# Loading the last 128 positions as tiles of 64 positions of two batches, masked by batch, with the second 64 positions scanned last

## The chip, the cores and the metric

The kernel runs on one core of one Trainium2 chip. The metric is the device time of an execution in microseconds, as the median of several; the executions of one kernel in one set agree within 0.15%. A profile's span, from the first to the last instruction, is 1.8 us shorter than the time in the kernel before. Ratios are the mean time of one kernel's fast runs over that of the other's fast runs in the same rounds, so they are not quite the ratio of the medians quoted.

## The reference

```python
B, S, D = 8, 2048, 4096              # x: [B, S, D] fp32, w: [D, 1] fp32
proj = (x @ w).squeeze(-1)           # [8, 2048]
cm = np.maximum.accumulate(proj, axis=1)
is_record = (proj >= cm).astype(np.float32)
return np.cumsum(is_record, axis=1)
```

x has 268 MB and each element is used once: a stream. Maximum and count run along the positions, so the last positions can only be finished once everything before them is.

## The kernel before

Positions 0 to 1919 come in four groups of 4, 4, 4 and 3 times 128 positions, the first three in a loop. In a group, each of the eight batches has a tile of 128 partitions with 4 (or 3) rows of 16 KB each. DVE takes the dot product of the first 2816 columns of a row, POOL multiplies the other 1280 by w and ACT sums them. Matmuls against the identity turn the sums into rows of positions, and DVE scans them. The last 128 positions follow as one tile per batch, the last two batches cut in pieces so that little work is left when the last bytes land.

```python
identity = sb([P, P], "identity")                 # 512 bytes per partition
small = sb([P, 352], "small")                     # 1408
w2 = sb([P, WC], "w2")                            # 2048
xall = sb([P, NS * R * D], "xall")                # 196608: three slots of 4 rows of 16 KB
xbuf = [xall[:, i * R * D : (i + 1) * R * D] for i in range(NS)]
w_sb = sb([P, PC], "w_sb")
# ... cm, cnt, cm_l, cnt_l (the last two 512 bytes each)

# the last two batches: batch, columns loaded, DVE's columns, POOL's columns
PIECES = [
    (1, 1408, D, (1408, VC), (VC, D)),
    # ... six pieces cut ...
    (0, 160, 448, (160, 448), None),
    (0, 0, 160, (0, 160), None),
]

def row_load(m, c0, c1, b, done):                 # one batch, 128 positions
    u, xb = slot(m)
    i = SY.dma_start(out=xb[:, c0:c1], in_=x[b, S0:, c0:c1]).then_inc(done, 16)
    # ... waits until the slot is free ...

with V.Fori(0, NL):                               # NL = 3
    next_group()
    group_dots(R)
next_group()
group_dots(RS[-1], NL)

# the end
        if i == len(PIECES) - 1:
            V.wait_ge(pa, na)                     # all of ACT's sums are there
# ...
V.tensor_reduce(out=fin, in_=accs, op=ALU.add, axis=mybir.AxisListType.X)
# ... matmuls of 128 columns into ps ...
scans(cm_l, cnt_l, P, cm[:, n - 1 : n], cnt[:, n - 1 : n], 4)
SY.dma_start(out=out[:, S0:], in_=cnt_l)
```

Of the kernel before, what the change touches and what calls it, by code (L numbers as in the profile page):

```python
# [13 lines left out]
ALU = mybir.AluOpType  # L14
ACTF = mybir.ActivationFunctionType
# [5 lines left out]
def kernel(  # L21
# [16 lines left out]
    P = 128  # L38
    B, S, D = x.shape
    WC = 512  # L40
    NW = D // WC
    RS = (4, 4, 4, 3)
    R = RS[0]
    NS = 3
    NG = len(RS)
    NL = NG - 1
    N = R * P
    STARTS = [sum(RS[:g]) * P for g in range(NG)]
    S0 = sum(RS) * P
    assert S0 + P == S  # L50
    VC = 2816
# [1 line left out]
    CV = 3584  # L53


    PIECES = [
        (1, 1408, D, (1408, VC), (VC, D)),
        (1, 0, 1408, (0, 1408), None),
        (0, 2816, D, (2816, 3328), (3328, D)),
        (0, 2048, 2816, (2048, 2816), None),  # L60
        (0, 1280, 2048, (1600, 2048), (1280, 1600)),
        (0, 832, 1280, (832, 1280), None),
        (0, 448, 832, (448, 832), None),
        (0, 160, 448, (160, 448), None),
        (0, 0, 160, (0, 160), None),
    ]
    W2 = 1280

    pool = ctx.enter_context(tc.tile_pool(name="sb", bufs=1))
    wpool = ctx.enter_context(  # L70
# [3 lines left out]
    def sb(shape, name, **kw):  # L74
        return pool.tile(shape, FP32, name=name, **kw)

    identity = sb([P, P], "identity")
    small = sb([P, 352], "small")
    w2 = sb([P, WC], "w2")
    xall = sb([P, NS * R * D], "xall")  # L80
    xbuf = [xall[:, i * R * D : (i + 1) * R * D] for i in range(NS)]
    w_sb = sb([P, PC], "w_sb")
    cm = sb([B, N], "cm")
    cnt = sb([B, N], "cnt")
    cm_l, cnt_l = (sb([B, P], n) for n in ("cm_l", "cnt_l"))
    w_v = wpool.tile([P, CV], FP32, name="w_v")
    ps = wpool.tile([P, WC], FP32, name="ps")
    w_row = w2[:NW, :]

    off = [0]  # L90

    def cut(n):
        off[0] += n
        assert off[0] <= 352
        return small[:, off[0] - n : off[0]]

    sum_v, sum_p = cut(R * B), cut(R * B)
    st_v, st_p = cut(B), cut(B)
    b1x = cut(B)
    accs = cut(2 * len(PIECES))  # L100
    acc_v, acc_p = accs[:, : len(PIECES)], accs[:, len(PIECES) :]
    fin = cut(1)
    neg = cut(1)[:B]

# [2 lines left out]
    def sem(name):  # L107
        return tc.alloc_semaphore(f"{name}_{next(ns)}")

    rows = [b for b in reversed(range(B)) if b > 1]  # L110
    xs = [sem("xs") for _ in range(B)]
    fr = [sem("fr") for _ in range(B)]
    xt = [sem("xt") for _ in rows]
    xq = [sem("xq") for _ in PIECES]
    ws, idn, bw, wc, cs, od, oe, psr, pd, pl, go, sd, pa, con = (
        sem(n) for n in "ws idn bw wc cs od oe psr pd pl go sd pa con".split()
    )

    V, A, G, T, SY = nc.vector, nc.scalar, nc.gpsimd, nc.tensor, nc.sync

    def dot(xsl, wsl, dst):
        return V.tensor_tensor_reduce(  # L122
            out=xsl, in0=xsl, in1=wsl, scale=1.0, scalar=0.0,
            op0=ALU.mult, op1=ALU.add, accum_out=dst,
        )
# [4 lines left out]
    def w_pool(c0, c1):  # L130
        if c0 >= VC:
            return w_sb[:, c0 - VC : c1 - VC]
        assert W2 <= c0 and c1 <= W2 + WC
        return w2[:, c0 - W2 : c1 - W2]

    def scans(cm_, cnt_, n, cm0, cnt0, base=1):
        low = neg.to_broadcast([B, n])
        V.tensor_tensor_scan(  # L138
            out=cm_, data0=ps[:B, :n], data1=low, initial=cm0, op0=ALU.max, op1=ALU.max,
        )._wait_ge(psr, base).then_inc(psr, 1)  # L140
        V.tensor_tensor(  # L141
            out=ps[:B, :n], in0=ps[:B, :n], in1=cm_, op=ALU.is_ge
        )._wait_ge(psr, base + 1).then_inc(psr, 1)
        V.tensor_tensor_scan(  # L144
            out=cnt_, data0=ps[:B, :n], data1=low, initial=cnt0, op0=ALU.add, op1=ALU.max,
        )._wait_ge(psr, base + 2).then_inc(cs, 1)

    def at(g, t):
# [9 lines left out]
    with tc.tile_critical(no_gpsimd_drain=True):  # L158

        for g in range(NG):  # L160
            r = RS[g]
            for t in range(B):
                i = SY.dma_start(
                    out=at(g, t)[:, : r * D],
                    in_=x[B - 1 - t, STARTS[g] : STARTS[g] + r * P, :].rearrange(
                        "(p r) d -> p (r d)", r=r
                    ),
                ).then_inc(xs[t], 16)
# [12 lines left out]
        def slot(m):  # L181
            if m < NS:
                return None, xbuf[m][:, RS[-1] * D :]
            u = B - NS if m < 2 * NS else B - NS + 1
            return u, at(NL, u)[:, (m % NS) * D : (m % NS + 1) * D]

        freed = {None}

        def row_load(m, c0, c1, b, done):
            u, xb = slot(m)  # L190
            i = SY.dma_start(  # L191
                out=xb[:, c0:c1], in_=x[b, S0:, c0:c1]
            ).then_inc(done, 16)
            if u not in freed:
                freed.add(u)
                i._wait_ge(fr[u], 2 * NG)

        for m, b in enumerate(rows):
            row_load(m, 0, D, b, xt[m])
        for i, (b, c0, c1, _, _) in enumerate(PIECES):  # L200
            row_load(B - 1 - b, c0, c1, b, xq[i])
            if i == 3:
                SY.dma_start(
                    out=out[:, STARTS[-1] : S0], in_=cnt[:, : S0 - STARTS[-1]]
                )._wait_ge(cs, NG + 1).then_inc(oe, 16)
# [22 lines left out]
        A.copy(out=w_sb[:, : CV - VC], in_=w_v[:, VC:CV])._wait_ge(bw, NW).then_inc(  # L228
            wc, 1
        )  # L230
        A.copy(out=w2, in_=w_v[:, W2 : W2 + WC]).then_inc(wc, 1)  # L231
        A.sem_inc(od, 32)


        V.memset(cm[:, N - 1 :], NEG)
        V.memset(cnt[:, N - 1 :], 0.0)
        V.wait_ge(con, 3)
# [3 lines left out]
        def group_scans(r=R):  # L241
            V.wait_ge(od, 16)
            n = r * P
            scans(cm[:, :n], cnt[:, :n], n, cm[:, N - 1 :], cnt[:, N - 1 :])

        def group_dots(r, g=0):
            for t in range(B):
                b, xb = B - 1 - t, at(g, t)
                V.wait_ge(xs[t], 16).then_inc(go, 1)
                V.sem_inc(xs[t], -16)  # L250
                for j in range(r):
                    i = dot(
                        xb[:, j * D : j * D + VC], w_v[:, :VC],
                        sum_v[:, j * B + b : j * B + b + 1],
                    )
                i.then_inc(fr[t], 1)

        def next_group():
            group_scans()
            V.sem_inc(psr, -3)  # L260
            V.sem_inc(od, -16)

        with V.Fori(0, NL):
            next_group()
            group_dots(R)
        next_group()
        group_dots(RS[-1], NL)

# [41 lines left out]
                        i.then_inc((pd, psr)[k], 1)  # L310


        nv = npool = na = 0
        parts = []

        def piece(xb, v, p, dst_v, dst_p, landed):
            nonlocal nv, npool, na
            dot(xb[:, v[0] : v[1]], w_v[:, v[0] : v[1]], dst_v)._wait_ge(
                landed, 16
            ).then_inc(sd, 1)  # L320
            nv += 1
            if p:
                xl = xb[:, p[0] : p[1]]
                G.tensor_mul(out=xl, in0=xl, in1=w_pool(*p))._wait_ge(  # L324
                    landed, 16
                ).then_inc(pl, 1)
                npool += 1
                add_up(xl, dst_p)._wait_ge(pl, npool).then_inc(pa, 1)
                na += 1

        for m, b in enumerate(rows):
            piece(
                slot(m)[1], (0, VC), (VC, D), st_v[:, b : b + 1], st_p[:, b : b + 1],
                xt[m],
            )
            if m == 0:
                group_scans(RS[-1])
        for i, (b, c0, c1, v, p) in enumerate(PIECES):
            if b == 1:
                dst_v, dst_p = (b1x if p is None else st_v)[:, 1:2], st_p[:, 1:2]  # L340
            else:
                dst_v, dst_p = acc_v[:, i : i + 1], acc_p[:, i : i + 1]
            piece(slot(B - 1 - b)[1], v, p, dst_v, dst_p, xq[i])
            if i == len(PIECES) - 1:
                V.wait_ge(pa, na)
            if i == 1:
                parts += [(B, st_v, (sd, nv)), (B, b1x, None), (B, st_p, (pa, na))]
        V.tensor_reduce(  # L348
            out=fin, in_=accs, op=ALU.add, axis=mybir.AxisListType.X
        )._wait_ge(sd, nv).then_inc(sd, 1)  # L350
        nv += 1
        parts.append((1, fin, (sd, nv)))
        for k, (m, l, wait) in enumerate(parts):
            i = T.matmul(  # L354
                out=ps[:m, :P], lhsT=l[:, :m], rhs=identity,
                start=k == 0, stop=k == len(parts) - 1,
            )
            if wait:
                i._wait_ge(*wait)
        i.then_inc(psr, 1)  # L360
        n = RS[-1] * P
        scans(cm_l, cnt_l, P, cm[:, n - 1 : n], cnt[:, n - 1 : n], 4)
        SY.dma_start(out=out[:, S0:], in_=cnt_l)._wait_ge(cs, NG + 2).then_inc(oe, 16)
        G.wait_ge(oe, 16 * 2)


# [28 lines left out]
```

## Time and profile before

| what | value |
|---|---|
| time | 631.46 us, median of 3 runs (631.19 to 631.63) |
| span of the profile | 629.5 us |
| DMA | 268.55 MB, 427 GB/s over the span |
| busy: DVE, POOL, ACT | 65%, 59%, 28% |
| last piece of x complete | 624.14 us |
| output issued | 626.98 us |

These lines are of the page of the kernel before: its span; the mean busy share of the 16 DMA engines in 40 slices, in tenths; packets and bytes; and one group of instructions (line, engine, operation, operands, count, then busy us and the mean ns of one, then the idle time before it).

```profile
span 629.5 us, 1144 instructions
...
DMA  9999999999999999999999999999999999999995
...
DMA packets 6868, 268.55 MB, mean 427 GB/s; under 512 B 800, under 2 KB 1328, under 8 KB 1872
...
L138 DVE TENSOR_TENSOR_SCAN cm_l<-ps,cm,small 8x128 f32<-8x128 f32 x1 | 0.5, 470 | 0.7 <-PE ps L354 0.7
```

The DMA row says what bounds the kernel: in every slice but the last the DMA engines are busy for 90% or more, while the busiest compute engine has a third of the span to spare. The last line is one of the scans that the change halves: 470 ns for 128 columns.

The next lines are the timeline of the kernel before: start us, duration us, engine, line, operation, operands, and in brackets the idle time before it with what ended it. First one of POOL's products, that of the sixth of the last tiles, then the end.

```profile
614.22 2.90 POOL L324 TENSOR_TENSOR xall<-xall,w_sb 128x1280 f32<-128x1280 f32 x1 [1.94 <-DMA xall<-in_x_dram]
...
624.45 0.32 DVE L122 CUSTOM_DVE_ANT_0 xall<-xall,w_v 128x160 f32<-128x160 f32 x1
624.69 0.08 DVE L122 DVE_READ_ACCUMULATOR2_ANT small<- 128x1 f32 x1
624.80 0.17 DVE L348 TENSOR_REDUCE small<-small 128x1 f32<-128x18 f32 x1
625.03 0.09 PEld L354 LDWEIGHTS ps<-identity,small 128*1 128x1 f32 x2 [3.14 <-DVE small L348]
625.03 0.58 PE L354 MATMUL ps<-identity,small 128*1 128x128 f32 x2 [2.65 <-DVE small L348]
625.65 0.47 DVE L138 TENSOR_TENSOR_SCAN cm_l<-ps,cm,small 8x128 f32<-8x128 f32 x1 [0.68 <-PE ps L354]
626.15 0.29 DVE L141 TENSOR_TENSOR ps<-ps,cm_l 8x128 f32<-8x128 f32 x1
626.48 0.47 DVE L144 TENSOR_TENSOR_SCAN cnt_l<-ps,cnt,small 8x128 f32<-8x128 f32 x1
626.98 0.31 SPq L363 DMA_DIRECT2D out_dram<-cnt_l  x1
```

POOL waits for the load and starts as it lands (here 1.94 us of waiting, the last share at 614.15 us and the start at 614.22). The end is a chain of small steps.

The trace also records each DMA packet and each of the 16 shares in which a load lands (the last piece has 128 packets and 16 landings, so a share is taken to be what one DMA queue brings, eight partitions). A load is complete with its last share. For the last piece of x, the ninth of the 16 shares landed at 622.57 us and the last at 624.14: one queue ended 1.58 us behind the middle of the others. (In this text a "queue" is one of these 16.)

### The profile page before, as it was taken

To read this page: it belongs to the slowest core of one execution; us is meant where nothing else is said; L and a number is where in the kernel's file an instruction comes from. 1 tells how busy PE (TensorE), PEld (TensorE's weight loads), DVE (VectorE), ACT (ScalarE), POOL (GpSimd) and SP (SyncE) were. 2 spreads that over 40 slices of the span, in tenths; PEclk is the share of its full clock that TensorE was granted. 3 is DMA by queue.
4 is the path that set the end of the run, shared out by engine and by line. 5 is a ranking of instruction groups with operands and counts; after the bars stand their busy time and mean duration, and the time that the engine had idled before them with its cause. 6 is when DMAs were issued, how large, how long until landed. Compare 5 with 4: busy or idle time off the path is not lost.

```text
span 629.5 us, 1144 instructions
## 1 busy us (share of the span) xinstructions
PE 29.7 (5%) x84; PEld 13.2 (2%) x84; DVE 406.2 (65%) x292; ACT 177.8 (28%) x262; POOL 368.8 (59%) x137
## 2 busy tenths in 40 slices
PE   8000000000010000000020000000002000000101
PEld 3000000000000000000010000000001000000000
DVE  0755676456785557755579655677557966555887
ACT  1222332123322233222233222332222322322332
POOL 0555676456765557755567655577555966555855
PEclk9999999999975555555555555555555555555555
DMA  9999999999999999999999999999999999999995
GB/s 401 400 466 404 462 400 467 400 466 400 466 400 466 400 466 421 447 416 450 433 433 446 421 458 408 459 408 458 408 416 450 441 412 447 441 415 443 415 432 220
DMA packets 6868, 268.55 MB, mean 427 GB/s; under 512 B 800, under 2 KB 1328, under 8 KB 1872
## 3 DMA queue, kind: packets, MB, share of 16 engines
q1 hardware_dynamic: 6848, 268.50, 98.8%
q14 instruction: 4, 0.03, 0.0%
q10 hardware_dynamic: 16, 0.02, 0.0%
HBM read 268.45 MB, written 0.07 MB: 427 GB/s over the span
## 4 chain that ended last, share of the span: by engine, by line
POOL 52%; issue 37%; DMA 7%; PE 2%; DVE 1%; SPq 0%; POOLq 0%; ACT 0%; ACTq 0%
POOL xall L273 52%; DMA xall<-in_x_dram 6%; PE w_v L221 2%; DVE xall L122 0%; PE ps L221 0%; SPq L191 0%; DMA w<-in_w_dram 0%; POOLq L276 0%; ACT w L231 0%; PE ps L354 0%; DVE cm_l L138 0%; DVE cnt_l L144 0%; DVE ps L141 0%; ACT xall L128 0%; DVE small L348 0%
## 5 line engine op out<-in xcount | busy, mean ns | idle before, releaser
L122 DVE CUSTOM_DVE_ANT_0 xall<-xall,w_v 128x2816 f32<-128x2816 f32 (+3 forms) x135 | 388.7, 2931 | 187.8 <-DVEq L250 184.9
L273 POOL TENSOR_TENSOR xall<-xall,w_sb 128x1280 f32<-128x1280 f32 x120 | 344.8, 2905 | 246.0 <-POOLq L276 246.0
L128 ACT ACTIVATE xall<-xall 128x1280 f32<-128x1280 f32 x129 | 162.6, 1261 | 431.2 <-POOL xall L273 412.4
L303 PE MATMUL ps<-identity,small 128*8 128x128 f32 x60 | 13.4, 418 | 566.6 <-ACT xall L128 566.6
L324 POOL TENSOR_TENSOR xall<-xall,w_sb 128x1280 f32<-128x1280 f32 (+1 forms) x8 | 22.1, 2769 | 7.6 <-DMA xall<-in_x_dram 7.6
L128 ACT ACTIVATION_READ_ACCUMULATOR xall<-xall 128x1 f32 x129 | 24.1, 186 | 0.0
L303 PEld LDWEIGHTS ps<-identity,small 128*8 128x8 f32 x60 | 7.5, 131 | 573.6 <-ACT xall L128 569.7
L138 DVE TENSOR_TENSOR_SCAN cm<-ps,cm,small 8x512 f32<-8x512 f32 (+1 forms) x5 | 6.1, 1217 | 13.5 <-PE ps L303 13.4
L221 PE MATMUL w_v<-w,identity 8*128 8x512 f32 x14 | 12.2, 1056 | 0.0
L239 DVE MEMSET ps<- 8x512 f32 x1 | 0.5, 485 | 17.4 <-ACT w L231 17.4
L122 DVE DVE_READ_ACCUMULATOR2_ANT small<- 128x1 f32 x135 | 11.0, 81 | 0.0
L144 DVE TENSOR_TENSOR_SCAN cnt<-ps,cnt,small 8x512 f32<-8x512 f32 (+1 forms) x5 | 6.1, 1217 | 0.2
L221 PEld LDWEIGHTS w_v<-w,identity 8*128 8x128 f32 x14 | 4.6, 332 | 7.3 <-issue 7.3
L228 ACT COPY w_sb<-w_v 128x768 f32<-128x768 f32 x1 | 0.8, 798 | 11.4 <-PE w_v L221 11.4
L354 PE MATMUL ps<-identity,small 128*8 128x128 f32 (+1 forms) x8 | 2.2, 405 | 26.4 <-DVE small L122 23.8
L141 DVE TENSOR_TENSOR ps<-ps,cm 8x512 f32<-8x512 f32 (+1 forms) x5 | 3.3, 660 | 0.2
L221 PE MATMUL ps<-w,identity 8*128 8x512 f32 x2 | 2.1, 1137 | 2.9 <-DMA w<-in_w_dram 2.9
L227 ACT ACT_TABLE_LOAD x1 | 1.3, 1283 | 1.5 <-SPq L158 1.5
L227 ACT COPY w_sb<-ps 128x512 f32<-128x512 f32 x1 | 0.6, 585 | 2.2 <-PE ps L221 2.2
L354 PEld LDWEIGHTS ps<-identity,small 128*8 128x8 f32 (+1 forms) x8 | 0.6, 100 | 28.1 <-DVE small L122 24.3
L324 POOL TENSOR_TENSOR xall<-xall,w 128x320 f32<-128x320 f32 x1 | 0.9, 867 | 0.1
L138 DVE TENSOR_TENSOR_SCAN cm_l<-ps,cm,small 8x128 f32<-8x128 f32 x1 | 0.5, 470 | 0.7 <-PE ps L354 0.7
(15 smaller groups left out, 3.5 us busy)
## 6 DMA issues: line engine op xcount, KB each, us to landing
xall<-in_x_dram SPq DMA_DIRECT2D x8, 6144.0 KB, 33.4
xall<-in_x_dram SPq DMA_DIRECT2D x6, 2048.0 KB, 43.0
xall<-in_x_dram SPq DMA_DIRECT2D x1, 1344.0 KB, 37.7
xall<-in_x_dram SPq DMA_DIRECT2D x2, 384.0 KB, 31.1
xall<-in_x_dram SPq DMA_DIRECT2D x1, 704.0 KB, 39.0
xall<-in_x_dram SPq DMA_DIRECT2D x1, 640.0 KB, 40.0
xall<-in_x_dram SPq DMA_DIRECT2D x24, 44.9
xall<-in_x_dram SPq DMA_DIRECT2D x1, 224.0 KB, 22.6
```

The lines of the kernel that those rows point to most:

```text
L122: return V.tensor_tensor_reduce(out=xsl, in0=xsl, in1=wsl, scale=1.0, scalar=0.0, op0=ALU.mult, op1=ALU.add, accum_out=dst,)
L128: return A.activation(out=xsl, in_=xsl, func=ACTF.Copy, accum_out=dst)
L138: V.tensor_tensor_scan(out=cm_, data0=ps[:B, :n], data1=low, initial=cm0, op0=ALU.max, op1=ALU.max,)._wait_ge(psr, base).then_inc(psr, 1)
L141: V.tensor_tensor(out=ps[:B, :n], in0=ps[:B, :n], in1=cm_, op=ALU.is_ge)._wait_ge(psr, base + 1).then_inc(psr, 1)
L144: V.tensor_tensor_scan(out=cnt_, data0=ps[:B, :n], data1=low, initial=cnt0, op0=ALU.add, op1=ALU.max,)._wait_ge(psr, base + 2).then_inc(cs, 1)
L221: i = T.matmul(out=dst, lhsT=identity[:NW, k : k + 1].to_broadcast([NW, P]), rhs=w_row, start=True, stop=True,).then_inc(bw, 1)
L227: A.copy(out=w_sb[:, CV - VC :], in_=ps)._wait_ge(bw, 1).then_inc(wc, 1)
L228: A.copy(out=w_sb[:, : CV - VC], in_=w_v[:, VC:CV])._wait_ge(bw, NW).then_inc(wc, 1)
L273: i = G.tensor_mul(out=xl, in0=xl, in1=w_sb).then_inc(pl, 1)
L303: i = T.matmul(out=ps[:B, j : r * P : r], lhsT=l[:, j * B : (j + 1) * B], rhs=identity, start=k == 0, stop=k == 1,)
L324: G.tensor_mul(out=xl, in0=xl, in1=w_pool(*p))._wait_ge(landed, 16).then_inc(pl, 1)
L354: i = T.matmul(out=ps[:m, :P], lhsT=l[:, :m], rhs=identity, start=k == 0, stop=k == len(parts) - 1,)
```

## The change

Each of the last tiles now holds 64 positions of two batches in place of 128 positions of one. Tiles 0 to 3 bring the first 64 positions of all eight batches, so these can be scanned while the rest loads, and only 64 columns are left to scan at the end. A partition's sum has to go to the row of its own batch: it is multiplied by a mask of zeros and ones over the batches (by ACT, and for the last tile by DVE), and a matmul with a folded identity turns the two batches into rows of 64 columns. The pieces were cut anew (the last is 352 columns, not 160), and the third DVE group was taken out of the loop.

```diff
-    PIECES = [ ... nine pieces of batches 1 and 0 ... ]
-    W2 = 1280
+    H = 2
+    Q = P // H
+    LAST = [
+        (B - 2, 1696, D, (1696, VC), (VC, D)),
+        (B - 2, 0, 1696, (0, 1696), None),
+        (B - 1, 2592, D, (2592, 3552), (3552, D)),
+        (B - 1, 1440, 2592, (1792, 2592), (1440, 1792)),
+        (B - 1, 736, 1440, (736, 1184), (1184, 1440)),
+        (B - 1, 352, 736, (352, 736), None),
+        (B - 1, 0, 352, (0, 352), None),
+    ]
+    EARLY = 4
+    W2, W2C = 1184, 608
@@ the tiles in SBUF
     identity = sb([P, P], "identity")
     small = sb([P, 352], "small")
-    w2 = sb([P, WC], "w2")
+    masked = sb([P, 2 * P], "masked")
+    fold = sb([P, 2 * B - H + Q], "fold")
+    w2 = sb([P, W2C], "w2")
     xall = sb([P, NS * R * D], "xall")
@@ the loads
-                out=xb[:, c0:c1], in_=x[b, S0:, c0:c1]
+                out=xb[:, c0:c1],
+                in_=x[
+                    rows_of(m)[0] : rows_of(m)[0] + H,
+                    S0 + rows_of(m)[1] : S0 + rows_of(m)[1] + Q, c0:c1,
+                ].rearrange("b i d -> i b d"),
@@ DVE's groups
-        with V.Fori(0, NL):
+        with V.Fori(0, NL - 1):
             next_group()
             group_dots(R)
+        next_group()
+        group_dots(R)
         next_group()
         group_dots(RS[-1], NL)
@@ the masks
+        def by_batch(m, acc, start, stop, *wait):
+            ...
+            if m < B - 1:
+                A.activation(out=e, in_=on, func=ACTF.Copy, scale=acc)...
+            else:
+                V.tensor_tensor(out=e, in0=on, in1=acc.to_broadcast([P, B]), op=ALU.mult)...
+            return T.matmul(out=ps[:B, q : q + Q], lhsT=e, rhs=by_i, start=start, stop=bool(stop))...
@@ the end (cut)
-        scans(cm_l, cnt_l, P, cm[:, n - 1 : n], cnt[:, n - 1 : n], 4)
+        by_batch(B - 1, fin, False, True, sd, nv).then_inc(psr, 1)
+        ne = EARLY * H * Q // B
+        tail_scans(EARLY, B, cm_l[:, ne - 1 : ne], cnt_l[:, ne - 1 : ne], 7)
```

More of the change, by code (lines that the diff above doesn't have):

```diff
@@ L53, with rows_of @@
     CV = 3584
-    PIECES = [
-        (1, 1408, D, (1408, VC), (VC, D)),
-        (1, 0, 1408, (0, 1408), None),
-        (0, 2816, D, (2816, 3328), (3328, D)),
-        (0, 2048, 2816, (2048, 2816), None),
-        (0, 1280, 2048, (1600, 2048), (1280, 1600)),
-        (0, 832, 1280, (832, 1280), None),
-        (0, 448, 832, (448, 832), None),
-        (0, 160, 448, (160, 448), None),
-        (0, 0, 160, (0, 160), None),
-    ]
-    W2 = 1280
+    H = 2
[8 more added lines that the diff above has]
+        (B - 1, 0, 352, (0, 352), None),
+    ]
+    def rows_of(m):
+        return m * H % B, m * H // B * Q
+    TILES = [(m, 0, D, (0, VC), (VC, D)) for m in range(B - 2)] + LAST
+    NP = sum(q[0] == B - 1 for q in LAST)
+    EARLY = 4
+    W2, W2C = 1184, 608
     pool = ctx.enter_context(tc.tile_pool(name="sb", bufs=1))
@@ L87 @@
     ps = wpool.tile([P, WC], FP32, name="ps")
-    w_row = w2[:NW, :]
+    w_row = w2[:NW, :WC]
+    by_b, by_i = fold[:, : 2 * B - H], fold[:, 2 * B - H :]
     off = [0]
@@ L97 @@
     sum_v, sum_p = cut(R * B), cut(R * B)
-    st_v, st_p = cut(B), cut(B)
-    b1x = cut(B)
-    accs = cut(2 * len(PIECES))
-    acc_v, acc_p = accs[:, : len(PIECES)], accs[:, len(PIECES) :]
+    acc_v, acc_p = cut(B + 1), cut(B)
+    accs = cut(2 * NP)
     fin = cut(1)
@@ L108, in sem @@
         return tc.alloc_semaphore(f"{name}_{next(ns)}")
-    rows = [b for b in reversed(range(B)) if b > 1]
     xs = [sem("xs") for _ in range(B)]
     fr = [sem("fr") for _ in range(B)]
-    xt = [sem("xt") for _ in rows]
-    xq = [sem("xq") for _ in PIECES]
-    ws, idn, bw, wc, cs, od, oe, psr, pd, pl, go, sd, pa, con = (
-        sem(n) for n in "ws idn bw wc cs od oe psr pd pl go sd pa con".split()
+    xq = [sem("xq") for _ in TILES]
+    ws, idn, bw, wc, cs, od, oe, psr, pd, pl, go, sd, pa, con, fo, ms = (
+        sem(n) for n in "ws idn bw wc cs od oe psr pd pl go sd pa con fo ms".split()
     )
@@ L132, in w_pool, with scans @@
             return w_sb[:, c0 - VC : c1 - VC]
-        assert W2 <= c0 and c1 <= W2 + WC
+        assert W2 <= c0 and c1 <= W2 + W2C
         return w2[:, c0 - W2 : c1 - W2]
-    def scans(cm_, cnt_, n, cm0, cnt0, base=1):
-        low = neg.to_broadcast([B, n])
+    def scans(cm_, cnt_, src, cm0, cnt0, base=1):
+        low = neg.to_broadcast(list(src.shape))
         V.tensor_tensor_scan(
-            out=cm_, data0=ps[:B, :n], data1=low, initial=cm0, op0=ALU.max, op1=ALU.max,
+            out=cm_, data0=src, data1=low, initial=cm0, op0=ALU.max, op1=ALU.max,
         )._wait_ge(psr, base).then_inc(psr, 1)
         V.tensor_tensor(
-            out=ps[:B, :n], in0=ps[:B, :n], in1=cm_, op=ALU.is_ge
+            out=src, in0=src, in1=cm_, op=ALU.is_ge
         )._wait_ge(psr, base + 1).then_inc(psr, 1)
         V.tensor_tensor_scan(
-            out=cnt_, data0=ps[:B, :n], data1=low, initial=cnt0, op0=ALU.add, op1=ALU.max,
+            out=cnt_, data0=src, data1=low, initial=cnt0, op0=ALU.add, op1=ALU.max,
         )._wait_ge(psr, base + 2).then_inc(cs, 1)
@@ L187 @@
         freed = {None}
-        def row_load(m, c0, c1, b, done):
+        for i, (m, c0, c1, _, _) in enumerate(TILES):
             u, xb = slot(m)
-            i = SY.dma_start(
-                out=xb[:, c0:c1], in_=x[b, S0:, c0:c1]
-            ).then_inc(done, 16)
+            d = SY.dma_start(
+                out=xb[:, c0:c1],
[3 more added lines that the diff above has]
+                ].rearrange("b i d -> i b d"),
+            ).then_inc(xq[i], 16)
             if u not in freed:
                 freed.add(u)
-                i._wait_ge(fr[u], 2 * NG)
-        for m, b in enumerate(rows):
-            row_load(m, 0, D, b, xt[m])
-        for i, (b, c0, c1, _, _) in enumerate(PIECES):
-            row_load(B - 1 - b, c0, c1, b, xq[i])
-            if i == 3:
+                d._wait_ge(fr[u], 2 * NG)
+            if i == len(TILES) - 4:
                 SY.dma_start(
@@ L230 @@
         )
-        A.copy(out=w2, in_=w_v[:, W2 : W2 + WC]).then_inc(wc, 1)
+        A.copy(out=w2, in_=w_v[:, W2 : W2 + W2C]).then_inc(wc, 1)
         A.sem_inc(od, 32)
+        V.wait_ge(idn, 1)
+        V.memset(by_b, 0.0).then_inc(fo, 1)
+        V.wait_ge(fo, 1)
+        V.tensor_reduce(
+            out=by_b[:, B - H : B], in_=identity.rearrange("p (i b) -> p b i", b=H),
+            op=ALU.add,
+            axis=mybir.AxisListType.X,
+        )
+        V.tensor_reduce(
+            out=by_i, in_=identity.rearrange("p (i b) -> p i b", b=H), op=ALU.add,
+            axis=mybir.AxisListType.X,
+        ).then_inc(fo, 1)
+        V.wait_ge(fo, 2)
         V.memset(cm[:, N - 1 :], NEG)
@@ L243, in group_scans @@
             n = r * P
-            scans(cm[:, :n], cnt[:, :n], n, cm[:, N - 1 :], cnt[:, N - 1 :])
+            scans(cm[:, :n], cnt[:, :n], ps[:B, :n], cm[:, N - 1 :], cnt[:, N - 1 :])
         def group_dots(r, g=0):
@@ L310, with sums @@
                         i.then_inc((pd, psr)[k], 1)
-        nv = npool = na = 0
-        parts = []
-        def piece(xb, v, p, dst_v, dst_p, landed):
+        nv = npool = na = nm = 0
+        def sums(i, dst_v, dst_p):
             nonlocal nv, npool, na
+            m, _, _, v, p = TILES[i]
+            xb = slot(m)[1]
             dot(xb[:, v[0] : v[1]], w_v[:, v[0] : v[1]], dst_v)._wait_ge(
-                landed, 16
+                xq[i], 16
             ).then_inc(sd, 1)
@@ L324, in piece @@
                 G.tensor_mul(out=xl, in0=xl, in1=w_pool(*p))._wait_ge(
-                    landed, 16
+                    xq[i], 16
                 ).then_inc(pl, 1)
@@ L329, in piece @@
                 na += 1
-        for m, b in enumerate(rows):
-            piece(
-                slot(m)[1], (0, VC), (VC, D), st_v[:, b : b + 1], st_p[:, b : b + 1],
-                xt[m],
-            )
+        def by_batch(m, acc, start, stop, *wait):
+            nonlocal nm
+            e = masked[:, nm * B : (nm + 1) * B]
+            b, q = rows_of(m)
+            on = by_b[:, B - H - b : 2 * B - H - b]
+            if m < B - 1:
+                A.activation(out=e, in_=on, func=ACTF.Copy, scale=acc)._wait_ge(
+                    *wait
+                ).then_inc(ms, 1)
+            else:
+                V.tensor_tensor(
+                    out=e, in0=on, in1=acc.to_broadcast([P, B]), op=ALU.mult
+                )._wait_ge(*wait).then_inc(ms, 1)
+            nm += 1
+            return T.matmul(
+                out=ps[:B, q : q + Q], lhsT=e, rhs=by_i, start=start, stop=bool(stop),
+            )._wait_ge(ms, nm)
@@ new lines, in tail_scans @@
+        def tail_scans(m0, m1, cm0, cnt0, base):
+            a, b = (m * H * Q // B for m in (m0, m1))
+            scans(cm_l[:, a:b], cnt_l[:, a:b], ps[:B, a:b], cm0, cnt0, base)
+        A.wait_ge(fo, 2)
+        n = RS[-1] * P
+        for i, (m, c0, _, _, p) in enumerate(TILES[: -NP]):
+            dv = acc_v[:, i : i + 1]
+            sums(i, dv, acc_p[:, m : m + 1])
+            if m in (0, EARLY):
+                T.wait_ge(cs, NG + 1 + (m > 0))
+            if p:
+                by_batch(m, acc_p[:, m : m + 1], rows_of(m)[0] == 0, False, pa, na)
+            mm = by_batch(m, dv, False, rows_of(m)[0] + H == B and c0 == 0, sd, nv)
@@ L336 @@
             if m == 0:
                 group_scans(RS[-1])
-        for i, (b, c0, c1, v, p) in enumerate(PIECES):
-            if b == 1:
-                dst_v, dst_p = (b1x if p is None else st_v)[:, 1:2], st_p[:, 1:2]
-            else:
-                dst_v, dst_p = acc_v[:, i : i + 1], acc_p[:, i : i + 1]
-            piece(slot(B - 1 - b)[1], v, p, dst_v, dst_p, xq[i])
-            if i == len(PIECES) - 1:
+            if m == EARLY - 1:
+                mm.then_inc(psr, 1)
+            if m == EARLY:
+                tail_scans(0, EARLY, cm[:, n - 1 : n], cnt[:, n - 1 : n], 4)
@@ L345 @@
+        for j in range(NP):
+            i = len(TILES) - NP + j
+            if j == NP - 1:
                 V.wait_ge(pa, na)
-            if i == 1:
-                parts += [(B, st_v, (sd, nv)), (B, b1x, None), (B, st_p, (pa, na))]
+            sums(i, accs[:, j : j + 1], accs[:, NP + j : NP + j + 1])
         V.tensor_reduce(
@@ L351 @@
         nv += 1
-        parts.append((1, fin, (sd, nv)))
-        for k, (m, l, wait) in enumerate(parts):
-            i = T.matmul(
-                out=ps[:m, :P], lhsT=l[:, :m], rhs=identity,
-                start=k == 0, stop=k == len(parts) - 1,
-            )
-            if wait:
-                i._wait_ge(*wait)
-        i.then_inc(psr, 1)
-        n = RS[-1] * P
-        scans(cm_l, cnt_l, P, cm[:, n - 1 : n], cnt[:, n - 1 : n], 4)
-        SY.dma_start(out=out[:, S0:], in_=cnt_l)._wait_ge(cs, NG + 2).then_inc(oe, 16)
+        by_batch(B - 1, fin, False, True, sd, nv).then_inc(psr, 1)
+        ne = EARLY * H * Q // B
+        tail_scans(EARLY, B, cm_l[:, ne - 1 : ne], cnt_l[:, ne - 1 : ne], 7)
+        SY.dma_start(out=out[:, S0:], in_=cnt_l)._wait_ge(cs, NG + 3).then_inc(oe, 16)
         G.wait_ge(oe, 16 * 2)
```

## The prediction

> **What bounds the kernel.** The x stream. The slice table shows DMA busy 9 tenths or more in 39 of 40 slices, 427 GB/s mean; DVE is busy 65%, POOL 59%. [...] (a 16 KB packet takes 0.611 us on each of 16 queues, 429 GB/s). The change loads the same bytes, so only the end can move. By the landing records the last piece (160 columns) is complete at 624.14 us; the span ends at 629.5.
>
> **The end before** (timeline): last dot starts 624.45, reduce 624.80, matmul 625.03, scans 625.65 to 626.95, output issued 626.98, 2.84 after the last landing.
>
> **What the change does there.**
> 1. Scans of 64 columns, not 128. From the 8x128 and 8x384 durations (0.47, 1.00 for a scan; 0.29, 0.55 for the compare) I estimate 0.34 and 0.23: 1.0 for the three instead of 1.33. Gain 0.33.
> 2. Last matmul: 64 columns, two passes of about 0.11 instead of 0.21. Gain 0.15 to 0.2.
> 3. A new masking multiply (128x8) on DVE between reduce and matmul. Loss 0.15 to 0.2.
> 4. The last piece is 352 columns, not 160: its dot is 0.2 longer. Loss 0.2.
> 5. The wait for ACT's sums before the last dot, which held nothing before, begins to bind: POOL's last product (256 columns) ends about 0.1 before the last landing, ACT's sum 0.4 after, so the last dot starts about 0.5 after landing (0.31 before). Loss 0.2.
> Sum: output issue again about 2.85 after landing. The gain is spent on 3 to 5.
> 6. Two fewer small loads: packet times (640 B 32 ns, 1152 B 51, 1536 B 65, 3072 B 121, against 611 for 16 KB), eight packets per queue, put the last landing about 0.15 earlier.
> 7. Two-batch tiles keep whole 16 KB rows: no change in rate expected. The early scan (about 1 us) follows the fifth tile's dot, where DVE idled 1.7 us: free. So are ACT's 15 small maskings.
>
> **The uncertain term: instruction fetch.** By the landing records one of 16 DMA queues lands its last share 1.0 us after the next slowest, 1.5 after most. Four 8 KB fetches happen in the run (104, 117, 492, 603 us)[...]. The slowest queue appears to have been hit twice. [...] The change unrolls one group on DVE (89 more instructions) and adds ACT and PE instructions, so fetches move; I can't tell whose they are. Same worst load: no change (likeliest); one less: 0.9 gained; one more: 0.9 lost. The unroll hints at a gain.
>
> **Prediction.** 631.2 us, 80% range 630.2 to 632.0. Faster by over 2%: 0.005; within 2%: 0.99; slower by over 2%: 0.005.
>
> **What would show it.** 427 to 428 GB/s over the span; last landing near 624.0 if fetches are neutral, near 623.1 or 624.9 if not; last dot about 0.5 after landing, behind ACT; scans 0.34, 0.23, 0.34; output issue 2.7 to 3.0 after landing. The gap between the slowest queue's landing and the next tells the fetch story.
>
> **What would make it wrong.** Two-batch sources slowing the 16 KB packets (0.611 us); a fetch that stalls an engine in the tail; DVE falling behind because the early scans wait for a mask on ACT.

Points 1 to 5 come to about nothing and point 6 to 0.15 us less, about 631.3 us from 631.46; the last 0.1 us to the forecast 631.2 is not itemized. What the trace of the kernel before shows of the fetches is the slowest queue's lag behind the ninth share: it rises from 0.25 to 0.70 us over those at 104 and 117 us, from 0.66 to 0.69 over that at 492, and from 0.71 to 1.66, by 0.95, over that at 603, near the 0.9 us of the forecast.

## The result, and the profile after

| | before | changed |
|---|---|---|
| time, median (range, runs) | 631.38 us (631.19 to 631.63, 4) | 633.44 us (633.25 to 633.79, 4) |
| ratio (95% interval) | | 1.0033 (1.0016 to 1.0050) |
| span of the profile | 629.5 | 631.6 |
| last piece: ninth share landed | 622.57 | 624.05 |
| last piece: last share landed | 624.14 | 626.02 |
| slowest queue behind the ninth | 1.58 | 1.97 |
| output issued (after the last share) | 626.98 (2.84) | 629.00 (2.98) |

The change costs 2.06 us, which is outside the predicted range. The lines of the page of the changed kernel that answer to those above:

```profile
span 631.6 us, 1212 instructions
...
DMA  9999999999999999999999999999999999999995
...
DMA packets 6581, 268.57 MB, mean 425 GB/s; under 512 B 768, under 2 KB 1040, under 8 KB 1584
...
q8 instruction: 1, 0.02, 0.0%
```

The rate has fallen from 427 to 425 GB/s although the DMA engines are as busy as before and fewer packets are small. The q8 line is a fetch of instructions that was not there before; it comes up below. The timeline of the changed kernel:

```profile
615.99 2.90 POOL L344 TENSOR_TENSOR xall<-xall,w_sb 128x1280 f32<-128x1280 f32 x1 [2.00 <-DMA xall<-in_x_dram]
...
626.60 0.52 DVE L127 CUSTOM_DVE_ANT_0 xall<-xall,w_v 128x352 f32<-128x352 f32 x1 [0.35 <-ACT xall L133]
627.04 0.08 DVE L127 DVE_READ_ACCUMULATOR2_ANT small<- 128x1 f32 x1
627.16 0.17 DVE L394 TENSOR_REDUCE small<-small 128x1 f32<-128x10 f32 x1
627.36 0.17 DVE L361 TENSOR_TENSOR masked<-fold,small 128x8 f32<-128x8 f32 x1
627.58 0.10 PEld L365 LDWEIGHTS ps<-fold,masked 128*8 128x8 f32 x2 [3.46 <-DVE masked L361]
627.58 0.38 PE L365 MATMUL ps<-fold,masked 128*8 128x64 f32 x2 [3.18 <-DVE masked L361]
628.00 0.34 DVE L143 TENSOR_TENSOR_SCAN cm_l<-ps,cm_l,small 8x64 f32<-8x64 f32 x1 [0.48 <-PE ps L365]
628.38 0.22 DVE L146 TENSOR_TENSOR ps<-ps,cm_l 8x64 f32<-8x64 f32 x1
628.63 0.34 DVE L149 TENSOR_TENSOR_SCAN cnt_l<-ps,cnt_l,small 8x64 f32<-8x64 f32 x1
629.00 0.31 SPq L401 DMA_DIRECT2D out_dram<-cnt_l  x1
```

Two readings follow. First, the end is about as forecast: the last dot waits for ACT (0.35 us), the mask takes 0.17, the scans 0.34, 0.22 and 0.34, and the output is issued 2.98 us after the last landing. Second, the sixth tile landed 1.77 us later (615.99 against 614.22). Most of the loss was there before the new end began. Further back, the ninth share of the first load of the fourth group landed at 481.80 us before and at 482.73 after. That is 0.93 us lost in loads that the change does not touch. Not all of it is lasting: 0.40 us was there by the fifth load (99.93 and 100.33), and in the second profiles of both kernels, taken on one chip, the difference at that later load is 0.35 us (481.95 and 482.30).

The packets say where. All have the sizes they had, and the medians of the three full sizes each rose:

| packet | before: median ns | changed: median ns | changed: 90th percentile |
|---|---|---|---|
| 64 KB (groups of four) | 2418 | 2420 | 2427 |
| 48 KB (group of three) | 1815 | 1818 | 1825 |
| 16 KB (last tiles) | 611 | 613 | 620 |

The extra is 2 to 3 ns at the median and 9 to 10 ns at the 90th percentile against the median before, for all three sizes. So something costs per packet, and not per byte. What the change did to all loads is to move their destination: with two new tiles and a longer one ahead of it, the x buffer starts at byte 22208 of each partition in the built program, where it started at 20480. 20480 is 80 times 256; 22208 is 192 bytes past a multiple of 256. (The diff gives the difference: 1720 bytes more of tiles ahead, and 8 of padding.)

### The profile page after: what moved, and what is told of

Its sections match the earlier page's. It is cut to its first block, busy times and chain, and to the rows that moved or that the text cites. A ratio compares the mean times of both kernels' runs of the same rounds, so it can differ in the third digit from the quotient of the medians.

```text
span 631.6 us, 1212 instructions
## 1 busy us (share of the span) xinstructions
PE 32.3 (5%) x108; PEld 14.4 (2%) x108; DVE 407.0 (64%) x295; ACT 182.0 (29%) x279; POOL 369.1 (58%) x138
## 4 chain that ended last, share of the span: by engine, by line
POOL 52%; issue 37%; DMA 7%; PE 2%; SPq 0%; DVE 0%; ACT 0%; POOLq 0%; ACTq 0%; DVEq 0%
POOL xall L292 52%; DMA xall<-in_x_dram 6%; PE w_v L225 2%; PE ps L225 0%; SPq L196 0%; DMA w<-in_w_dram 0%; POOL xall L344 0%; POOLq L295 0%; ACT xall L133 0%; ACT w L235 0%; DVE xall L127 0%; PE ps L365 0%; DVE cm_l L143 0%; DVE cnt_l L149 0%; DVE ps L146 0%
## 5 line engine op out<-in xcount | busy, mean ns | idle before, releaser
L133 ACT ACTIVATE xall<-xall 128x1280 f32<-128x1280 f32 (+1 forms) x130 | 162.9, 1253 | 425.5 <-POOL xall L292 415.1
L365 PE MATMUL ps<-fold,masked 128*8 128x64 f32 x32 | 5.2, 299 | 23.3 <-ACT masked L357 17.3
L357 ACT ACTIVATE masked<-fold,small 128x8 f32<-128x8 f32 x15 | 4.0, 296 | 4.1 <-DVE small L127 3.9
L365 PEld LDWEIGHTS ps<-fold,masked 128*8 128x8 f32 x32 | 1.9, 97 | 26.8 <-ACT masked L357 19.8
L344 POOL TENSOR_TENSOR xall<-xall,w 128x352 f32<-128x352 f32 (+1 forms) x2 | 1.6, 841 | 0.1
```

Of the source, the lines that this page charges most:

```text
L133: return A.activation(out=xsl, in_=xsl, func=ACTF.Copy, accum_out=dst)
L344: G.tensor_mul(out=xl, in0=xl, in1=w_pool(*p))._wait_ge(xq[i], 16).then_inc(pl, 1)
L357: A.activation(out=e, in_=on, func=ACTF.Copy, scale=acc)._wait_ge(*wait).then_inc(ms, 1)
L365: return T.matmul(out=ps[:B, q : q + Q], lhsT=e, rhs=by_i, start=start, stop=bool(stop),)._wait_ge(ms, nm)
```

## The experiments

Twelve kernels ran, all with correct results, in four sets, each set on one chip beside the kernel before. The theory is the destination address. Its rivals are a chip or run with slower memory, the two-batch source, and the unrolled DVE group. The table has the numbers; "9th" and "last" are the landing of the ninth and the last share of the last piece, "issue" is the output after the last landing.

| run | x buffer at | 16 KB packet, median / 90% ns | 9th | last | issue | span | time | ratio (95%) |
|---|---|---|---|---|---|---|---|---|
| before_again | 20480 | 611 / 611 | 622.73 | 624.30 | 2.85 | 629.7 | 631.52 | (one run) |
| after_again | 22208 | 613 / 620 | 623.64 | 625.66 | 2.96 | 631.2 | 633.58 | 1.0033 (1.0019 to 1.0046) |
| before_shifted | 22208 | 613 / 620 | 623.72 | 625.59 | 2.86 | 631.0 | 632.94 | 1.0022 (1.0009 to 1.0036) |
| after_aligned | 20480 | 611 / 611 | 622.80 | 624.22 | 2.96 | 629.7 | 631.89 | 1.0007 (0.9993 to 1.0020) |
| gap64 | 20544 | 613 / 620 | 623.71 | 626.05 | 2.86 | 631.5 | 632.93 | 1.0020 (1.0007 to 1.0034) |
| gap128 | 20608 | 615 / 619 | 623.91 | 625.75 | 2.87 | 631.2 | 632.99 | 1.0024 (1.0010 to 1.0038) |
| gap256 | 20736 | 611 / 611 | 622.56 | 624.26 | 2.85 | 629.7 | 631.48 | 0.9998 (0.9985 to 1.0012) |
| aligned_rolled | 20480 | 611 / 611 | 622.88 | 624.60 | 2.97 | 630.1 | 632.11 | 1.0007 (0.9993 to 1.0021) |
| aligned_tail | 20480 | 611 / 611 | 622.58 | 624.26 | 2.67 | 629.5 | 631.87 | 1.0001 (0.9988 to 1.0015) |
| even_groups | 20480 | 611 / 611 | 623.13 | 623.71 | 2.88 | 629.5 | 631.61 | 0.9999 (0.9985 to 1.0013) |
| even_changed | 20480 | 611 / 611 | 623.36 | 624.15 | 2.71 | 629.9 | 632.41 | 1.0011 (0.9998 to 1.0025) |
| even_mixed | 20480 | 611 / 611 | 623.37 | 623.82 | 2.89 | 629.3 | 631.33 | 0.9996 (0.9982 to 1.0010) |

The kernel before had medians of 631.58, 631.67, 631.63 and 631.46 us beside these (rows 1 to 4, 5 to 8, 9 to 11, and 12).

### before_again and after_again: the controls

No edit.

> Control: the kernel before, profiled on the chip of the other runs. Alignment theory (the x buffer starts at byte 22208 of each partition after the change instead of 20480, and every load packet gets a little dearer): packets of 64, 48 and 16 KB take 2418, 1815 and 611 ns at the median with almost no spread, half of the queues finish the last load by about 622.6 us, last landing 624.1, span 629.5. Rival (the two profiles came from chips or runs of different memory speed): the packets here are as dear as after the change, 613 to 620 ns for 16 KB, and half of the queues finish at about 624.

> Control: the changed kernel again. Ratio to before 1.003 to 1.0035 (633.4 us). Both theories: packets of 16 KB with a spread of 611 to 620 ns, last landing about 626.0, the slowest queue 1.9 to 2.0 us behind the median. If the slow queue's lag is run to run noise it should differ by several tenths from 1.97 us here.

Both came out as the address theory has it. On one chip the kernel before has 611 ns packets and the changed one 613 to 620, and the difference of 2 us stays. A slower chip is excluded as the cause.

### before_shifted: only the address

```diff
     w2 = sb([P, WC], "w2")
+    gap = sb([P, 432], "gap")
     xall = sb([P, NS * R * D], "xall")
```

> The kernel before with an unused tile of 1728 bytes ahead of the x buffer, so that the buffer starts at byte 22208, nothing else changed. Alignment theory: 16 KB packets 613 to 620 ns, the time rises by 1.2 to 1.5 us, ratio about 1.002, the median queue's last landing at about 624. Rival theories (two-batch source, unrolled DVE group, chip): ratio 1.0000 within 0.0003.

Measured: 632.94 us against 631.58, 1.36 us more, from an unused tile. The packets have the distribution of the changed kernel. The same product of POOL starts 1.05 us later than in before_again, the kernel before on the same chip (and 1.22 us later than in its first profile). The lines are of the timelines of before_again and before_shifted, in this order:

```profile
614.39 2.90 POOL L324 TENSOR_TENSOR xall<-xall,w_sb 128x1280 f32<-128x1280 f32 x1 [1.95 <-DMA xall<-in_x_dram]
...
615.44 2.90 POOL L325 TENSOR_TENSOR xall<-xall,w_sb 128x1280 f32<-128x1280 f32 x1 [2.01 <-DMA xall<-in_x_dram]
```

### after_aligned: the change without the shift

```diff
     small = sb([P, 352], "small")
     masked = sb([P, 2 * P], "masked")
+    cm_l, cnt_l = (sb([B, P], n) for n in ("cm_l", "cnt_l"))
+    xall = sb([P, NS * R * D], "xall")
     fold = sb([P, 2 * B - H + Q], "fold")
     w2 = sb([P, W2C], "w2")
-    xall = sb([P, NS * R * D], "xall")
```

> The changed kernel with two 512-byte tiles moved ahead of the x buffer and the new small tiles behind it, so that the buffer starts at byte 20480 again. Alignment theory: 16 KB packets at 611 ns, 1.2 to 1.5 us come back, ratio about 1.001 (632.0 us); what is left is the later end of the slowest queue (about 0.4) and the longer tail after landing (0.14). Rivals: 633.4 us stays.

Measured: 631.89 us, 1.69 us less than the changed kernel on the same chip, somewhat more than forecast. The stream is back where it was, as the timeline of after_aligned shows for the same product (614.22 before the change):

```profile
614.24 2.90 POOL L344 TENSOR_TENSOR xall<-xall,w_sb 128x1280 f32<-128x1280 f32 x1 [1.97 <-DMA xall<-in_x_dram]
```

Its 16 KB packets, all from two-batch sources, take 611 ns each: the two-batch source costs nothing. What is left against the kernel before is 0.31 us, and the interval of the ratio holds 1. The spans do not show it: 629.7 us in both profiles of this chip, after_aligned and before_again. It lies outside the span (see below).

### gap64, gap128, gap256: which boundary

The edit is that of before_shifted, with `gap` of 16, 32 and 64 columns (64, 128 and 256 bytes).

> The kernel before with a 64-byte unused tile ahead of the x buffer (start at byte 20544, a multiple of 64 but not of 128). If any start off a 256-byte boundary costs: 16 KB packets of 613 ns at the median and 620 in some queues, ratio 1.002. If 64-byte alignment were enough: 611 ns, ratio 1.000; but then the shifted kernel, whose buffer also started at a multiple of 64, should not have been slower, so this is unlikely.

> The same with 128 bytes (start 20608). If the boundary that matters is 256 bytes: packets as dear as with 1728 bytes (613 to 620 ns for 16 KB), ratio 1.002, 632.9 us. If it is 128 bytes: 611 ns and 631.6 us.

> The same with 256 bytes (start 20736, a multiple of 256 but not of 512). If the boundary is 256 bytes: 611 ns, 631.6 us, ratio 1.000. If it is 512 bytes or more: 613 to 620 ns and 632.9 us.

The two starts off a multiple of 256 cost 1.26 and 1.32 us; the start at 20736, a multiple of 256 but not of 512, costs nothing. For these loads the boundary is 256 bytes: the 16 KB packets take 611 ns at the median with the starts 20480 and 20736, and 613, 615 and 613 with 20544, 20608 and 22208. The medians at 64 and at 192 bytes past the boundary are equal, 613 ns. In these runs the source did not move and the destination did. By what mechanism this costs was not shown.

One rival was not tested by a run: that it is not the destination's start that counts, but whether source and destination lie equally far past a 256-byte boundary. For whole rows the two are the same, since each row of x starts a multiple of 256 bytes into x. Some of the last pieces start 128 bytes past a boundary in their row, and their packets in the traces speak for the rival:

| packet | run | bytes past a boundary: source (from the start of x), destination | ns, mean |
|---|---|---|---|
| 1536 bytes | before | 0, 0 | 65.0 |
| 1536 bytes | after_aligned | 128, 128 | 65.0 |
| 1152 bytes | before | 128, 128 | 51.0 |
| 1152 bytes | gap128 | 128, 0 | 52.6 |

In these packets a destination off the boundary costs nothing where the source is as far off, and one on the boundary costs where the source is off it. How much a difference costs varies from packet to packet: in before_shifted 36 of the 768 packets of 16 KB took the old 611 ns, 373 took 613 and 146 took 620. Why is open.

The loss builds up with the packets. Against before_again, the ninth share in before_shifted is 0.03 us later at the first load, 0.33 after the groups of four (192 packets per queue), 0.59 after the group of three (64 more), 0.81 after the six whole tiles (48 more) and 0.99 at the last piece. As an estimate, a packet of 64 KB costs 1.6 ns more, one of 48 KB 4.1 and one of 16 KB 4.6; the last two are near the rise of the packets' own means (4.6 and 4.0 ns), while the mean of the 64 KB packets did not rise (2423.5 and 2423.6), as both runs hold some slow ones. The last share moved by 1.29 us. The other 0.30 is the slowest queue. It is 1.84 to 2.34 us behind the ninth in all five profiles with a shifted buffer, and 1.42 to 1.72 in the six of the same groups with an aligned one; why is open.

### aligned_rolled: the unrolled DVE group

```diff
-        with V.Fori(0, NL - 1):
+        with V.Fori(0, NL):
             next_group()
             group_dots(R)
-        next_group()
-        group_dots(R)
```

(on top of after_aligned)

> The changed kernel with its buffer at byte 20480 and the third DVE group put back into the loop (89 DVE instructions fewer). Theory: the DVE queue's second instruction fetch goes from 491 us to the tail (about 603 us) and costs that queue 1 us there instead of earlier; [...] the last landing is the same, 624.2 within 0.2, and the time 631.9 within 0.2. Rival one: the unroll is what keeps the changed kernel behind, and the rolled one is faster by 0.3 us or more. Rival two: a fetch in the tail hurts more than an earlier one, and the rolled one is slower by 0.5 us or more.

The fetch moved as forecast, from 491 to 603 us. The last landing is 624.60, 0.4 us later than in after_aligned and so twice as far off as I allowed; the slowest queue is 1.72 us behind, against 1.42 in after_aligned. But aligned_tail, which has the unrolled group too, shows 1.68, so this differs as much between runs of unrolled kernels. The time is 0.22 us more, of two kernels on different chips whose ratios to the kernel before are the same, 1.0007. So by the medians neither rival shows at the size named for it; but the interval of each ratio is 0.13% (0.8 us) to each side, so neither is excluded.

### aligned_tail: the wait before the last dot

```diff
-        (B - 1, 736, 1440, (736, 1184), (1184, 1440)),
+        (B - 1, 736, 1440, (736, 1312), (1312, 1440)),
```

(on top of after_aligned)

> The changed kernel with its buffer at byte 20480, and POOL's share of the third-last load cut from 256 to 128 columns (DVE's from 448 to 576). It tests the wait for ACT's sums before the last dot: if that wait holds the last dot, ACT ends about 0.4 us earlier, the last dot starts about 0.25 after the last landing instead of 0.56, and the output is issued about 2.65 us after landing instead of 2.96; time 631.6. If the wait is not what holds it, the last dot starts later than before, by the 0.13 us that DVE's longer dot takes.

The last dot starts 0.28 us after the last landing (624.54 and 624.26) and waits for nothing; the output is issued 2.67 us after landing. The timeline of aligned_tail:

```profile
624.54 0.52 DVE L127 CUSTOM_DVE_ANT_0 xall<-xall,w_v 128x352 f32<-128x352 f32 x1
...
626.93 0.31 SPq L401 DMA_DIRECT2D out_dram<-cnt_l  x1
```

So the wait cost 0.3 us of the shorter scan's gain, and with it gone the new end is 0.17 to 0.18 us shorter than the old one (2.84 and 2.85). In the time this does not show: the median is 631.87, not the 631.6 expected, and the ratio is 1.0001 with an interval of 0.13% to each side. In the spans it does: they are 629.58 us in the mean, against 629.90 in the kernel before beside it. What is lost again lies outside the span.

### even_groups, even_changed, even_mixed: instruction fetch

The records of the kernel before hold four instruction fetches after the start, single packets of 8 KB that take 0.31 us each (at 104, 117, 492 and 603 us). Around those at 492 and 603 us one queue has a gap of 0.30 us and then a packet 0.22 and 0.53 us longer than usual. After the last of them the slowest queue goes from 0.71 to 1.66 us behind the ninth, and it is still 1.58 behind at the end. In the changed kernel the second hit on a queue comes at 492 us instead, the lag goes from 1.02 to 1.99 us, and a 16 KB fetch (1.07 us) appears at 619 us, on another queue: the lag of the second slowest goes from 0.82 to 1.34 us and that of the slowest stays at 2.0 to 2.1. Since it was DVE's program that grew at that place and the fetch came earlier, it is taken to be DVE's; aligned_rolled, where it moved back with DVE's program, agrees. The 16 KB fetch is taken to be TensorE's, which has 24 more matmuls: it stays in even_changed, where the programs of DVE, POOL and ACT are shorter. The trace names no engine for a fetch. To remove it, DVE's program was made shorter:

```diff
-    RS = (4, 4, 4, 3)
+    RS = (3, 3, 3, 3, 3)
+    ROWS = 4                     # rows per slot, in place of R
-        with V.Fori(0, NL):
+        with V.Fori(0, NG):
             next_group()
             group_dots(R)
-        next_group()
-        group_dots(RS[-1], NL)
# POOL's and ACT's loops likewise; slots are the same in every group
```

> The kernel before with five groups of three rows, all in the loops, in place of three groups of four in the loop and one of three behind it: 128 DVE instructions instead of 215, 64 on ACT instead of 105, the same arithmetic and the same bytes. Instruction fetch theory: the second fetch on DVE's queue (603 us) is gone, so the slowest queue ends 0.8 us or less behind the median instead of 1.6, the last landing is at 623.3 to 623.6 instead of 624.2, and the time is 630.6 to 630.9, ratio 0.9987. Rival: the queue that is 1.6 us late is slow of itself, the lag stays, and the time stays at 631.6; or the smaller loads starve the DMA queues and it is slower.

> The changed kernel with its buffer at byte 20480, five groups of three rows in the loops, and the smaller last POOL share. TensorE's 16 KB fetch at 617 us (it is there in every version with the 16 masked matmuls) should remain and make its queue 0.9 to 1.3 us late, now the slowest: last landing about 623.8, output issue 2.65 after it, time 631.0 to 631.3. If the fetch theory is wrong, as aligned_tail.

The lag fell as the fetch theory has it, to 0.58 us in even_groups. But the ninth share came 0.4 us later than in before_again (623.13 and 622.73): the groups now move in 48 KB packets, and four of these (7260 ns) take longer than three of 64 KB (7254), with more packets in all. So the last landing improved by 0.6 us, not 1.0. And the time did not improve at all. The span did, by 0.4 us in the mean (629.50 and 629.90), though POOL's clearing of the semaphores, the program's closing step, came 2.33 us after the output was issued (1.96 in the kernel before). What is outside the span grew by 0.33 us, and two 8 KB instruction fetches came there, after the last instruction; that they cause it is not shown. In even_changed the 16 KB fetch taken to be TensorE's stayed, at 617 us, and set the slowest queue (0.79 us behind); it landed at 624.15 rather than the 623.8 expected, had the late closing step too, and is 0.8 us slower than the kernel before by the medians (the interval just holds 1).

even_mixed keeps only DVE's groups all in the loop and takes POOL's and ACT's last group out of it again. It tests whether the late closing step and the two late fetches go with the shorter programs of these two.

> As even_groups, but only DVE keeps all five groups in its loop; POOL's and ACT's last group stands behind the loop again, so that these two programs are about as long as in the kernel before. In even_groups the last landing was 0.4 to 0.6 us earlier than in the kernel before and the time the same: at the end POOL's closing instruction came 0.36 us late, and two 8 KB instruction fetches came only after the last instruction. [...] Expected: last landing near 623.7, no fetch after the output, span 629.1, time 631.1 to 631.3. If the theory is wrong: fetches after the output stay and the time is 631.6; or one queue is hit twice again and the landing is back at 624.2.

The closing step is back at 1.96 us after the issue, and of the two late fetches one moved into the run (516 us) and one stayed behind the end; that the fetches set the closing step is not shown. The landing is 623.82 and the time 631.33 us against 631.46: a gain of 0.13 us by the medians, which the interval doesn't tell from none (its span is 0.44 us shorter in the mean, and 0.23 of that is lost outside it). No version here is proved faster than the kernel before.

## Why the prediction was wrong

**The step that failed** is the first: "The change loads the same bytes, so only the end can move", repeated in point 7 as "no change in rate expected". The bytes were the same and the new source cost nothing; the destination had moved. The two new tiles stand ahead of the x buffer and put it off a 256-byte boundary, and the large packets of the whole run pay some 2 to 10 ns each. The term had been taken as 0, with 427 to 428 GB/s forecast; the rate was 425. It measures 1.36 us by shifting the kernel before and 1.69 us by undoing the shift in the changed one, of the 2.06 us lost. The evidence lay in the diff and in the sizes of the tiles; I had not added them up.

**Outside the span** lies a second loss that the forecast has no term for, and it has nothing to do with the address. Each run has its time and its span (to 0.1 us); the difference is 1.79 us in the mean in the kernel before, and the same in before_shifted, gap64, gap128 and gap256 (1.78 to 1.83). In the changed kernel it is 2.16, and 2.17, 2.18, 2.15 and 2.19 in after_again, after_aligned, aligned_rolled and aligned_tail. That is about 0.37 us more in each of these kernels, and enough for the 0.31 us that after_aligned is slower: its mean span is that of the kernel before to 0.03 us (629.82 and 629.79). The cause is open; the traces show no difference between the kernels in that time.

**The end (points 1 to 5)** was right in sum and in parts. Forecast: output 2.85 us after the last landing, last dot about 0.5 after it behind ACT, scans 0.34, 0.23, 0.34, mask 0.15 to 0.2. Measured: 2.98, 0.58, 0.34, 0.22, 0.34, 0.17 us. That the shorter scan's gain was spent on the mask, the longer last dot and the wait is shown by the timeline, and for the wait by aligned_tail.

**Earlier landing through fewer small loads (point 6)**, 0.15 us, is not seen: with the address restored the ninth share lands at 622.58 to 622.88 in the runs of the changed kind and at 622.56 to 622.73 in the kernels of before. Runs differ by as much as the gain, so it is neither shown nor excluded.

**The early scan and ACT's masks (point 7)** are free, as forecast: before the sixth tile POOL still waits 2.00 us for the load, and DVE has 0.9 us idle.

**Instruction fetch.** The likeliest case, no change in the worst queue, holds where the address is restored (1.42 to 1.72 us behind the ninth, against 1.58 before). In the changed kernel the worst queue was 0.4 us further behind (1.97 and 2.02), of which before_shifted, with the address alone, shows 0.3. The fetch taken to be DVE's second moved from 603 to 492 us, and the lag rises by 0.97 us at 492 in the changed kernel and by 0.95 at 603 in the one before. The queue hardly caught up: it was 1.60 us behind at 496 us and 1.42 at the end in after_aligned, and 1.66 at 603 us and 1.58 at the end in the kernel before. The new fetch that I had left open as possible is the one of 16 KB; it hit another queue and did not set the end in the changed kernel.

What stays open: what takes 0.37 us outside the span; and why the cost of a packet off the boundary changes from packet to packet.

## What to carry to other kernels

In a kernel whose DMA engines are busy throughout, as here (90% or more in 39 of 40 slices), look at the start address of the buffer that takes the stream whenever a tile is added ahead of it, and try a start on a 256-byte boundary, by allocating it first or padding what stands before it: here a start off it cost 1.26 to 1.36 us, 0.2% of the time. (With a source that is itself off the boundary, the small packets above suggest the same distance past it instead, 51.0 ns against 52.6; test that.) The difference that built up here over loads that the change doesn't touch was a cost per packet; compare packet times of equal size between the two traces before explaining the end. Subtract the span from the time in every run: in even_groups a span 0.4 us shorter met 0.33 us more outside it. And a step shortened at the end of a chain can buy nothing until the wait that takes its place is moved too: here the output was issued 2.96 us after the last landing with that wait (after_aligned) and 2.67 without it (aligned_tail), against 2.84 before the change.
